# Activations and weights in two DMA queues at the start of a two-block network

## The chip, the core and the metric

The kernel runs on one NeuronCore of a Trainium2 chip. Its engines are TensorE (matrix products, PE in the profile; PEld is its loading of stationary operands), VectorE (DVE), ScalarE (ACT), GpSimd (POOL) and SyncE (SP, which here only issues DMAs). The metric is the device time of one execution in microseconds, less is better; the median of three runs is compared.

## The reference

For one sequence of 256 tokens of width 1024 in float32, two blocks run one after the other. The first has two layers: retention with four heads, then causal latent attention, each with a gated addition of a side input. The second has a gated convolution branch, a pooling branch and a feed-forward part. Only the very beginning matters here:

```
h = rms_norm(x, pre_norm_g[0])
z = h @ ret_w_in            # columns: q, k, v, gate
v = z[..., 2048:4096]       # four heads of 512 columns
q = rope(q, positions); k = rope(k, positions) / 16
```

rms_norm divides each token's row by the root of its mean square and multiplies by a gain per channel. The kernel multiplies by the gain first, and divides after the product, since the division is by token.

## The kernel before, in words

Activations are held transposed: 128 channels in the partitions, 256 tokens along the free dimension, so that x is eight blocks of 128 x 256 (`xt`, in two tiles of four blocks). Weights come as 128 x 128 or 128 x 512 blocks, packed on the host in the order of use into tiles of 128 x 1024 (512 KB), and are fetched by `fetch` (line 162, tile `raw`). For most products each operand is split in a rounded high part and a low rest, and three products of the fast float32 format (lines 234 to 236, `mm`) stand for one. The split of a weight tile is line 175 on ScalarE (`wh`, the high part) and line 176 on VectorE (`wl`, the rest). The split of an activation block with its gain is line 187 on ScalarE and line 188 on VectorE.

The first product is v of head 0 (`ret_v(0)`). Its eight weight blocks of 128 x 512 lie in four raw tiles of two blocks each. The first tile is not split: blocks 0 and 1 of x, times the gain (`xg`, line 497 on VectorE), meet the raw weights in full float32 products (line 240, `mm32`), for which the profile has two instructions each. For blocks 2 to 7 the split forms are used:

```
for kb in range(f):                                   # f = 2, full float32
    for b in range(2):
        mm32(psv[b], xg[kb][:, b * P:(b + 1) * P], v0raw[kb // 2][...], kb == 0, False)
for kb in range(f, 8):                                # three products each
    w = seq.next()                                    # splits the next raw tile
    for b in range(2):
        mm(psv[b], (xp[0][kb][:, bs], xp[1][kb][:, bs]), w, kb == 0, kb == 7)
```

Before the first product TensorE multiplies a tile of ones by itself nine times into a bank that nobody reads (line 273). The squares of x are taken in pairs of blocks on ScalarE (line 295), added on VectorE (line 299) and summed over the partitions by TensorE (line 359). `vec` is one tile of 458 columns with all gains, biases and small vectors; its first 16 columns are `pre_norm_g`. From the other columns, six small VectorE instructions (lines 661, 731, 732 and three of line 944) make scaled copies for later use, and the last two columns hold the rotary frequencies (line 441).

All early loads go out from SP in this order: vec, blocks 0 and 1 of x, the two halves of the first weight tile, blocks 2 and 3, the second weight tile, blocks 4 and 5, blocks 6 and 7, the third weight tile, the positions. They are held in program order. The order of all other instructions on each engine is settled at build time by a planner that weighs priorities, operands and expected times; on the chip each engine then runs its list strictly in that order. An instruction waits for the regions of a tile that it reads, not for the whole tile.

The profile calls loads of x `half<-in_xT`, loads of weights `raw<-in_wts`.

Of the kernel before, what the change touches and what calls it, by code (L numbers as in the profile page):

```python
# [21 lines left out]
D = 1024  # L22
# [60 lines left out]
def tile_kernel(ctx, tc, order, xT, pT, pos, vec, cst, cv, wada, wts, outT):  # L83
    nc = tc.nc
# [11 lines left out]
    def nm(s):  # L96
        uid[0] += 1
        return f"{s}_{uid[0]}"

    def bank():  # L100
        return pp.tile([P, 512], F32, tag="bank", name=nm("ps"))
# [52 lines left out]
    def fetch(entries, width, parts=True, step=D, pinned=False):  # L154
        g = len(order)
        order.append((width, list(entries)))
        n = len(entries) * width
        tag, bufs = (("raw", 6), ("wh", 5), ("wl", 5))[0 if parts else [0, 1][g % len([0, 1])]]
        raw = wp.tile([P, D], F32, tag=tag, name=nm("raw"), bufs=bufs)
        for o in range(0, n, step):  # L160
            e = min(n, o + step)
            d = nc.sync.dma_start(out=raw[:, o:e], in_=wts[g, :, o:e])
            if pinned:
                tc.keep_in_program_order(d)
        return raw[:, :n]
# [81 lines left out]
    xt = Blk(DB)  # L247
    vc = cp.tile([P, NV], F32, name="vec")
    posi = tp.tile([P, S], I32, tag="t1", name="posi", bufs=7)
    cs = cp.tile([P, NC], F32, name="cst")  # L250
    def load_x(q):
        tc.keep_in_program_order(nc.sync.dma_start(out=xt.pair(q), in_=xT[:, 2 * q:2 * q + 2, :]))


    v0 = [("ret_in", kb * P, 2048) for kb in range(8)]
    tc.keep_in_program_order(nc.sync.dma_start(out=vc, in_=vec))
    load_x(0)
    v0raw = []
    for q in range(3):
        v0raw.append(fetch(v0[2 * q:2 * q + 2], 512, q >= 1, 512 if q == 0 else D, True))  # L260
        if q < 2:
            load_x(q + 1)
        if q == 1:
            load_x(3)
    tc.keep_in_program_order(nc.sync.dma_start(out=posi, in_=pos.partition_broadcast(P)))
    ident = cp.tile([P, P], F32, name="ident")
    make_identity(nc, ident)
# [1 line left out]
    V.memset(ones, 1.0)  # L269

    wu = bank()
    for _ in range(9):
        T.matmul(wu[:, :P], ones, ones, start=True, stop=True)
    eps_r = cp.tile([P, 1], F32, name="eps_r")
    V.memset(eps_r, RMS_EPS)
# [387 lines left out]
    def post(x, ys, sums, layer, prepared):  # L663

        x1 = Blk(DB)

        def scaled(ks):
            for k in ks:
                A.activation(x1[k], ys.at(k), AF.Copy, scale=pgh[:, layer * 8 + k:layer * 8 + k + 1])
        scaled(range(3))  # L670
        nry = rms_neg2(sums.ps[0], D)
        scaled(range(3, DB))
        prj = prepared()
        x1p = two(DB)
        for k, n in ((0, 1), (1, 1), (2, 2), (4, 2), (6, 1), (7, 1)):
            V.tensor_mul(x1.span(k, n), x1.span(k, n), bc2(nry, n))
            V.tensor_add(x1.span(k, n), x1.span(k, n), x.span(k, n))
            split(x1p[0].span(k, n), x1p[1].span(k, n), x1.span(k, n))
        x2 = Blk(DB)

        def fin(ps, k, n):
            sgm = t2()[:, :n, :]
            A.activation(sgm, ps, AF.Sigmoid)
            V.tensor_mul(sgm, sgm, prj.span(k, n))
            V.tensor_add(x2.span(k, n), sgm, x1.span(k, n))

        half_outer(f"ple_gate{layer}", x1p, fin)
        return x2
# [38 lines left out]
    xt = post(xt, ys, sums, 0, prep)  # L727
# [200 lines left out]
    xt = post(xt, ys, sums, 1, prep)  # L928
# [508 lines left out]
```

## Time and profile before

| what | value |
|---|---|
| median of three runs | 865.53 us (865.46 to 867.07) |
| the profiled execution: its time | 866.75 us |
| its span, first to last instruction | 864.9 us |
| mean granted TensorE clock in it | 0.995 |
| PE busy | 848.1 us, 98% of the span |
| DVE busy | 710.0 us, 82% |
| ACT busy | 557.5 us, 64% |
| moved by DMA | 165.95 MB, 192 GB/s in the mean |

A row of a timeline has the start, the time taken, the engine, the line, the operation, what it writes and reads, and how many such instructions follow each other; in brackets the idle time of the engine before it and what ended that. In the chain of work that ended last, each piece starts when the one before it has released it. The granted clock of TensorE has two levels, 1.2 and 2.4 GHz. The column of the granted clock stands at 1.00 in the first microseconds too, where no change of the clock was recorded yet; what the engine had there is read from the spacing of equal instructions.

### The profile page before, as it was taken

How to read it: one execution, taken by the hardware profiler on the slowest of the kernel's cores; microseconds unless marked ns; L12 is line 12 of the kernel's file. 1: busy time of each engine (PE TensorE's matmuls, PEld its weight loads, DVE VectorE, ACT ScalarE, POOL GpSimd, SP SyncE). 2: the span in 40 equal slices, each digit the busy share in tenths (PEclk: the TensorE clock that was granted, in tenths of full speed). 3: DMA queues.
4: the chain of work that ended last, by engine and by line, in shares of the span. 5: the costliest groups of instructions: out<-in, count | busy, mean ns of one | idle time of the engine just before them, and what ended most of it. 6: DMA issues, size and time to landing. Idle time of an engine off the chain costs nothing.

```text
span 864.9 us, 16461 instructions
## 1 busy us (share of the span) xinstructions
PE 848.1 (98%) x6472; PEld 818.8 (95%) x6472; DVE 710.0 (82%) x1277; ACT 557.5 (64%) x943; POOL 4.2 (0%) x22
## 2 busy tenths in 40 slices
PE   8999999999999999999999999999999999999994
PEld 6989899999999999999999999999998999999993
DVE  6999787888888978799874768899776888889965
ACT  6665555445775785776744867998755776666533
POOL 0000000000000000000000000000000000000000
PEclk9999999999999999999999999999999999999997
DMA  9857556888556655465254364255473466567601
GB/s 333 314 217 243 196 206 207 271 258 297 170 185 228 225 185 199 160 227 197 97 183 171 122 219 152 92 170 185 137 239 124 135 187 191 185 230 256 206 27 49
DMA packets 46461, 165.95 MB, mean 192 GB/s; under 512 B 5168, under 2 KB 5936, under 8 KB 46384
## 3 DMA queue, kind: packets, MB, share of 16 engines
q1 hardware_dynamic: 46224, 164.39, 56.0%
q8 instruction: 50, 0.82, 0.4%
q0 software_dynamic: 160, 0.52, 0.2%
q14 instruction: 27, 0.22, 0.1%
HBM read 163.85 MB, written 1.05 MB: 191 GB/s over the span
## 4 chain that ended last, share of the span: by engine, by line
PE 95%; DVE 2%; DMA 2%; ACT 0%; issue 0%; SPq 0%; DVEq 0%
PE ps L235 27%; PE ps L234 27%; PE ps L236 27%; PE ps L240 10%; PE ps L359 2%; PE ps L337 1%; DMA adach<-in_wada 1%; DMA half<-in_xT 1%; PE ps L895 1%; PE ps L194 1%; DVE wl L176 0%; DVE t L1233 0%; DVE t L1230 0%; PE ps L1143 0%; PE ps L1151 0%
## 5 line engine op out<-in xcount | busy, mean ns | idle before, releaser
L234 PE MATMUL ps<-half,wh 128*128 128x256 f32 x1680 | 474.5, 283 | 0.0
L235 PE MATMUL ps<-half,wh 128*128 128x256 f32 x1680 | 472.9, 282 | 0.1
L236 PE MATMUL ps<-half,wl 128*128 128x256 f32 x1680 | 471.3, 281 | 0.0
L175 ACT CAST wh<-raw 128x1024 fp32r<-128x1024 f32 x233 | 242.6, 1048 | 159.7 <-PE ps L235 121.1
L176 DVE TENSOR_TENSOR wl<-raw,wh 128x1024 fp32r<-128x1024 f32 x233 | 282.4, 1222 | 64.3 <-ACT wh L175 62.5
L235 PEld LDWEIGHTS ps<-half,wh 128*128 128x128 f32 x1680 | 316.4, 188 | 1.6 <-DVE half L185 0.7
L236 PEld LDWEIGHTS ps<-half,wl 128*128 128x128 f32 x1680 | 316.9, 189 | 0.0
L234 PEld LDWEIGHTS ps<-half,wh 128*128 128x128 f32 x1680 | 316.0, 188 | 0.8
L240 PE MATMUL ps<-half,raw 128*128 128x256 f32 (+2 forms) x384 | 84.9, 380 | 0.0
L240 PEld LDWEIGHTS ps<-half,raw 128*128 128x128 f32 x384 | 72.5, 190 | 10.0
L409 DVE CUSTOM_DVE_ANT_0 adach<-adach,siluc 128x1024 f32<-128x1024 f32 x48 | 58.5, 1222 | 18.1 <-DMA adach<-in_wada 18.1
L1060 ACT ACTIVATE t<-apad,vec 128x256 f32<-128x256 f32 x106 | 44.4, 499 | 0.9 <-DVE half L1061 0.9
L1061 DVE TENSOR_TENSOR half<-half,t 128x512 f32<-128x512 f32 x53 | 36.7, 693 | 4.1 <-ACT t L1060 1.8
L234 PE MATMUL ps<-wh,half 128*128 128x512 f32 (+1 forms) x92 | 33.5, 366 | 0.0
L184 ACT CAST half<-t 128x256 fp32r<-128x256 f32 (+1 forms) x47 | 20.6, 453 | 19.7 <-DVE t L1323 12.1
L235 PE MATMUL ps<-wl,half 128*128 128x512 f32 (+1 forms) x92 | 32.7, 355 | 0.5 <-DVE wl L176 0.5
L236 PE MATMUL ps<-wh,half 128*128 128x512 f32 (+1 forms) x92 | 32.6, 355 | 0.0
L185 DVE TENSOR_TENSOR half<-t,half 128x256 fp32r<-128x256 f32 (+1 forms) x47 | 21.8, 485 | 3.7 <-ACT half L184 2.9
L1318 ACT ACTIVATE t<-ps,vec 128x256 f32<-128x256 f32 x38 | 21.0, 557 | 3.6 <-DVE t L1320 2.4
L235 PEld LDWEIGHTS ps<-wl,half 128*128 128x128 f32 x92 | 17.4, 189 | 3.3 <-DVE wl L176 1.0
L234 PEld LDWEIGHTS ps<-wh,half 128*128 128x128 f32 x92 | 17.3, 189 | 3.1 <-ACT wh L175 0.9
L236 PEld LDWEIGHTS ps<-wh,half 128*128 128x128 f32 x92 | 17.3, 188 | 2.6
(261 smaller groups left out, 994.6 us busy)
## 6 DMA issues: line engine op xcount, KB each, us to landing
raw<-in_wts SPq DMA_DIRECT2D x257, 512.0 KB, 4.2
adach<-in_wada SPq DMA_DIRECT2D x48, 512.0 KB, 4.8
half<-in_xT SPq DMA_DIRECT2D x4, 256.0 KB, 6.9
cst<-in_cst SPq DMA_DIRECT2D x1, 928.0 KB, 10.0
raw<-in_wts SPq DMA_DIRECT2D x2, 256.0 KB, 4.5
siluc<-in_cv SPq DMA_DIRECT2D x1, 512.0 KB, 8.1
t<-in_pT POOLq DMA_DIRECT2D x2, 256.0 KB, 4.9
out<-half SPq DMA_DIRECT2D x4, 128.0 KB, 2.0
```

The lines of the kernel that those rows point to most:

```text
L175: A.copy(hi, raw)
L176: V.tensor_sub(lo, raw, hi.bitcast(F32))
L184: A.copy(hi, src)
L185: V.tensor_sub(lo, src, hi.bitcast(F32))
L234: T.matmul(ps, l[0], r[0], start=first, stop=False)
L235: T.matmul(ps, l[0], r[1], start=False, stop=False)
L236: T.matmul(ps, l[1], r[0], start=False, stop=last)
L240: T.matmul(ps, w, r, start=first, stop=last)
L409: V.tensor_tensor_reduce(ch, ch, sc, 1.0, 0.0, MUL, ADD, mod[:, n:n + 1])
L1060: A.activation(t[:, b, :], apad[:, i0 + b, k:k + S], AF.Copy, scale=w[b])
L1061: V.tensor_add(acc.pair(i0 // 2), acc.pair(i0 // 2), t)
L1318: A.activation(t[:, b, :], ps[:, b, :], AF.Identity, bias=col("b_dw_f_2", m), scale=w[2])
```

## The change

The loads of x move from SP's queue to the one of ScalarE, as five transfers: block 0, block 1, blocks 2 and 3, 4 and 5, 6 and 7. SP first loads the 16 columns of `vec` that hold `pre_norm_g`, then the three weight tiles (the first in two halves, as before), then the other 442 columns of `vec`, then the positions. TensorE does seven products of ones for nine.

```diff
-    def load_x(q):
-        tc.keep_in_program_order(nc.sync.dma_start(out=xt.pair(q), in_=xT[:, 2 * q:2 * q + 2, :]))
+    def load_x(k, n):
+        tc.keep_in_program_order(nc.scalar.dma_start(out=xt.span(k, n), in_=xT[:, k:k + n, :]))
 
     v0 = [("ret_in", kb * P, 2048) for kb in range(8)]
-    tc.keep_in_program_order(nc.sync.dma_start(out=vc, in_=vec))
-    load_x(0)
-    v0raw = []
-    for q in range(3):
-        v0raw.append(fetch(v0[2 * q:2 * q + 2], 512, q >= 1, 512 if q == 0 else D, True))
-        if q < 2:
-            load_x(q + 1)
-        if q == 1:
-            load_x(3)
+    tc.keep_in_program_order(nc.sync.dma_start(out=vc[:, :16], in_=vec[:, :16]))
+    for k, n in ((0, 1), (1, 1), (2, 2), (4, 2), (6, 2)):
+        load_x(k, n)
+    v0raw = [fetch(v0[2 * q:2 * q + 2], 512, q >= 1, 512 if q == 0 else D, True) for q in range(3)]
+    tc.keep_in_program_order(nc.sync.dma_start(out=vc[:, 16:], in_=vec[:, 16:]))
     tc.keep_in_program_order(nc.sync.dma_start(out=posi, in_=pos.partition_broadcast(P)))
...
     wu = bank()
-    for _ in range(9):
+    for _ in range(7):
         T.matmul(wu[:, :P], ones, ones, start=True, stop=True)
```

## Rows read from the trace of the kernel before

**Rows 1.** The page's part on the chain of work that ended last: its share of the span by engine.

```profile
PE 95%; DVE 2%; DMA 2%; ACT 0%; issue 0%; SPq 0%; DVEq 0%
```

**Rows 2.** The chain that ended last, in order of time, from 0 to 30 us: start, time taken, engine or DMA, tile and line.

```profile
2.59 6.37 DMA half<-in_xT
8.98 0.91 ACT half L187 x2
...
10.61 0.94 ACT wh L175
11.58 1.24 DVE wl L176
12.86 0.50 PE ps L235
...
15.43 1.81 PE ps L359 x8
```

**Rows 3.** Who waited for whom, TensorE's products, whole execution: engine, tile, line, what it waited for, us in total, times, longest.

```profile
PE ps L895 <- DVE sm L884: 1.0, 1, 1.0
PE ps L337 <- DVE t L346: 0.9, 1, 0.9
...
PE ps L235 <- DVE wl L176: 0.5, 1, 0.5
```

**Rows 4.** Timeline of TensorE's products, 0 to 16 us.

```profile
1.05 4.21 PE L273 MATMUL ps<-ones 128*128 128x128 f32 x18 [1.05 <-DVE eps_l L277]
6.06 5.50 PE L240 MATMUL ps<-raw,half 128*128 128x512 f32 x8 [0.80 <-DMA raw<-in_wts]
11.60 0.73 PE L234 MATMUL ps<-wh,half 128*128 128x512 f32 x2
```

**Rows 5.** Timeline of TensorE's loads of stationary operands, 0 to 13 us, four of line 240.

```profile
8.75 0.34 PEld L240 LDWEIGHTS ps<-raw,half 128*128 128x128 f32 x1 [0.52 <-issue]
9.60 0.26 PEld L240 LDWEIGHTS ps<-raw,half 128*128 128x128 f32 x1 [0.52 <-issue]
10.11 0.19 PEld L240 LDWEIGHTS ps<-raw,half 128*128 128x128 f32 x1 [0.24 <-issue]
10.54 0.19 PEld L240 LDWEIGHTS ps<-raw,half 128*128 128x128 f32 x1 [0.24 <-issue]
```

**Rows 6.** Timeline of SP's DMA issues, 0 to 60 us, the first ones.

```profile
0.74 0.38 SPq L256 DMA_DIRECT2D vec<-in_vec  x1
1.18 0.42 SPq L252 DMA_DIRECT2D half<-in_xT  x1
1.65 0.90 SPq L162 DMA_DIRECT2D raw<-in_wts  x2
2.59 0.43 SPq L252 DMA_DIRECT2D half<-in_xT  x1
3.06 0.43 SPq L162 DMA_DIRECT2D raw<-in_wts  x1
...
4.82 0.61 SPq L162 DMA_DIRECT2D raw<-in_wts  x1
```

**Rows 7.** The same loads one by one, each from the DMA view of the stretch that holds its issue alone, in the order of issue (at 0.74, 1.18, 1.65, 2.11, 2.59, 3.06 and 4.82 us): size, us from issue to landing.

```profile
vec<-in_vec SPq DMA_DIRECT2D x1, 229.0 KB, 2.5
half<-in_xT SPq DMA_DIRECT2D x1, 256.0 KB, 3.7
raw<-in_wts SPq DMA_DIRECT2D x1, 256.0 KB, 4.3
raw<-in_wts SPq DMA_DIRECT2D x1, 256.0 KB, 4.8
half<-in_xT SPq DMA_DIRECT2D x1, 256.0 KB, 6.4
raw<-in_wts SPq DMA_DIRECT2D x1, 512.0 KB, 7.2
...
raw<-in_wts SPq DMA_DIRECT2D x1, 512.0 KB, 8.1
```

**Rows 8.** Table by stretches, 2 to 9 and 9 to 13 us: stretch, length, busy time (and instructions) of PE, PEld, DVE, ACT and POOL, granted clock, busy share of the 16 DMA engines, GB/s.

```profile
2.00:9.00 7.00, 6.21 (x20) 4.39 (x19) 2.04 (x10) 1.65 (x6) 0.01 (x1) 1.00 0.91 283
9.00:13.00 4.00, 3.43 (x8) 1.18 (x8) 3.00 (x5) 4.00 (x9) 0.00 (x0) 1.00 1.04 414
```

**Rows 9.** Timeline of ScalarE, 0 to 24 us.

```profile
0.73 1.28 ACT L278 ACT_TABLE_LOAD   x1 [0.73 <-PEq L1420]
...
4.94 0.63 ACT L295 ACTIVATE t<-half 128x512 f32<-128x512 f32 x1 [2.72 <-DMA half<-in_xT]
...
8.98 0.91 ACT L187 ACTIVATE half<-half,vec 128x256 fp32r<-128x256 f32 x2 [2.61 <-DMA half<-in_xT]
...
10.51 1.03 ACT L175 CAST wh<-raw 128x1024 fp32r<-128x1024 f32 x1
11.45 1.70 ACT L187 ACTIVATE half<-half,vec 128x256 fp32r<-128x256 f32 x4
```

**Rows 10.** Timeline of VectorE, 0 to 24 us.

```profile
3.31 0.18 DVE L661 TENSOR_SCALAR pgh<-vec 128x16 f32<-128x16 f32 x1 [2.29 <-DMA vec<-in_vec]
...
3.53 0.31 DVE L944 TENSOR_SCALAR lng<-vec 128x8 f32<-128x8 f32 x3
...
9.52 0.89 DVE L188 SCALAR_TENSOR_TENSOR half<-half,vec,half 128x256 fp32r<-128x256 f32 x2 [2.64 <-ACT half L187]
```

## The prediction

> **What bounds the kernel now.** I read the shares of the chain that ended last first, since they tell whether the start can matter at all: 95% of it is TensorE [rows 1]. Then the waits of TensorE's products over the whole execution [rows 3]: after the first microseconds only two waits of note are left, 1.0 us at line 895 and 0.9 us at line 337, each behind a short chain of this kernel's own that moves with TensorE. So from the first split product on TensorE runs almost without a gap, and the kernel ends earlier by what that steady run starts earlier. Third, the chain through the first 30 us [rows 2]: the steady run starts at 12.86 us with the first line 235. Going back from there: the low part of the second weight tile (line 176, from 11.58), its high part on ScalarE (line 175, critical from 10.61, started 10.51 [rows 9]), ScalarE's work on blocks 2 and 3 of x from 8.98 on, and the load of these blocks, issued at 2.59 and 6.37 us under way. Two loads are nearly tied there: blocks 2 and 3 land at 8.99 (2.59 + 6.4), the second weight tile at 10.26 (3.06 + 7.2) [rows 6, 7]; the cast starts 0.25 us after that landing, because ScalarE still has line 187 and what follows it in its list.
>
> TensorE before that is not the bound. Its warm-up ends at 5.26, it waits 0.80 us for the first half tile of weights, runs the eight full float32 instructions from 6.06 to 11.56, and then does two line 234 and stops for the low part [rows 4]. The spacing of those eight tells the clock: 0.85 us from 8.75 to 9.60, 0.43 us from 10.11 to 10.54 [rows 5]. So the engine had 1.2 GHz until shortly after 9.60, after the warm-up, the gap of 0.80 and some 3.5 us of products, and 2.4 GHz from then on.
>
> Last, the loads. From 2 to 9 us the DMA engines are 91% busy and move only 283 GB/s, from 9 to 13 us 414 GB/s [rows 8]. So a load's landing follows from the bytes ahead of it, on a curve that is slow at first. In KB up to and with each load, and its landing from [rows 6, 7]: vec 229 at 3.24; blocks 0 and 1, 485 at 4.88; half tiles 741 at 5.95 and 997 at 6.91; blocks 2 and 3, 1253 at 8.99; second tile 1765 at 10.26; third tile, with 512 KB of x in between, 2789 at 12.92.
>
> **The change, part by part.**
>
> *The order of bytes.* 221 KB of vec go behind the third weight tile; 8 KB stay in front. The two queues share the engines. How they are mixed no row shows, so I bound it. Packets of x are half as wide as those of weights (128 KB against 256, 256 against 512 for as many rows), so if the engines alternate packet by packet from the same start, each load of x ends with the weight load next to it. Then the second weight tile has 8 + 512 + 256 + 512 + 256 = 1544 KB up to its end: 8.99 + 291 KB x 2.48 ns (slope between 1253 and 1765) = 9.71 us. If the small vec transfer holds SP back by one step, blocks 4 and 5 run beside it: 1800 KB, 10.35. I take the middle, 10.03 (before: 10.26). Blocks 2 and 3 land at 7.2 us in the second pairing (1032 KB) and at 9.7 in the first; the first half tile at 4.28 (392 KB) or 5.03 (520 KB), against 5.95.
>
> *From there to the steady run.* Cast start to first line 235 took 12.86 - 10.51 = 2.35 us, and that stays. If ScalarE is free, the cast starts 0.1 us after the landing. The bounds: 9.71 + 0.1 + 2.35 = 12.16 (gain 0.70); 10.35 + 0.1 + 2.35 = 12.80 (gain 0.06); and in the first pairing with the cast behind ScalarE's work on blocks 2 and 3 (10.51 - 8.98 = 1.53 us), 9.71 + 1.53 + 2.35 = 13.59 (loss 0.73). The middle, 10.03 + 0.1 + 2.35 = 12.48, gains 0.4 us, and this I take.
>
> *Two products of ones fewer.* Eighteen instructions took 4.21 us, the last starting near 4.84, so 0.223 us from one to the next; fourteen end near 4.4. The first weights come at 4.3 to 5.0, so TensorE starts its real products at 4.4 to 5.1, a gap of 0 to 0.7 us against 0.80 [rows 4]. From 5.1, with the clock rising at the same 9.7, eight instructions end at about 10.9 (5.4 at 0.853, 2.6 at 0.43); at 1.2 GHz throughout at 11.95. Both lie before 12.16. So this part costs and brings nothing by itself; it is covered by the wait for the second tile, and if that wait goes, each of those instructions left at the low clock costs 0.43 us.
>
> *Five issues on ScalarE.* At 0.43 us each, or up to 0.6 where issues back up [rows 6], they take 2.2 to 3 us before the table load (1.28 us, [rows 9]), so ScalarE is ready at about 4.4 to 5.2, not at 2.2. Its first work started at 4.94, after 2.72 us idle, and another 2.61 us idle stand before 8.98. Costed at nothing. Without that cover the split of blocks 0 and 1 is late, which TensorE does not read in this product.
>
> *Four issues fewer on SP, one more.* The second weight tile is issued near 2.1 for 3.06, the third near 2.5 for 4.82. With up to 7 to 8 us from issue to landing [rows 7], it is the bytes ahead that set the landing. Bytes up to the third tile and vec together are 2789 KB as before, so positions and everything behind them land as before.
>
> *Six small VectorE instructions.* They ran from 3.31 to 3.84 [rows 10] because vec was the first load. Their columns now land with 2789 KB, 12.92 us. So 0.53 us moves into a stretch in which VectorE is full. Cover: blocks 2 to 5 come earlier in half of the cases, and VectorE sat idle 2.64 us before 9.52 [rows 10]. I take nothing, with 0.53 us as the upper bound.
>
> The Trainium skill, page "DMA: Bandwidth & Descriptors", section "Issuing engines are not separate DMA queues", says that transfers of different issuing engines interleave on the same 16 DMA engines, and that a second issuer saves only issue time. By that rule the gain is that of the byte order alone, as summed above, and the second rival below does not exist. The row with 91% busy at 283 GB/s fits engines that are short of data rather than of work, and does not decide it [rows 8].
>
> **Sum.** The profiled execution has 866.75 us, of which 864.9 are the span; minus 0.4 gives 866.35. It lies 1.2 us above the median of the runs, so for the median I forecast 865.53 - 0.4 = 865.1 us. A change within 0.2% (1.7 us) is about what this kernel's runs cannot tell from none; their own spread is 1.6.
>
> **The rivals.**
>
> *Hidden by the sums.* TensorE's list has the sums of squares (line 359) at 15.43, on the chain [rows 2]. They need blocks 6 and 7, which end the queue of x at about 2568 KB, 12.35 us by the curve, while ScalarE's four line 187 ran from 11.45 [rows 9]. Then the sums come no earlier than now, and TensorE waits there for what it gained: 865.5.
>
> *The slow start is eased.* If a second queue lets the DMA engines overlap their slow first reads, and they move 414 GB/s instead of 283 over those 7 us, the same 1.98 MB take 4.8 us and the second tile lands 2.2 us sooner, 7.8. The steady run could start at 10.25, but the eight first products end at 10.5 to 10.9: gain 2.0, 863.5. Half of it gives 864.0. For it: the engines are slow while busy. Against: nothing shows that queues are what they lack.
>
> *VectorE blocked (slower).* If the six small instructions stand ahead of the first line 176 in VectorE's list, it waits for 12.92, does 0.53 us of them, starts line 176 at about 13.55 and TensorE at 14.83: 1.97 us later, 867.5. It decides from that place in the list alone; ahead of line 497 it would be over 4 us. For it: before, they stand ahead of all. Against: they stood there because vec was first.
>
> *The clock falls (slower).* TensorE is through at 9 to 10.9 and stands until 12.2 to 12.5 but for two products. If the clock falls to 1.2 GHz for as long as it was low after 6.06 (3.7 us), half is lost, 1.84 us: 865.1 + 1.8 = 867.0. Before, a shorter stop there left the clock high.
>
> **How the numbers follow.** Forecast 0.50 (its own range 864.8 to 866.3, from the bounds -0.70 and +0.73); hidden 0.14; eased start 0.20; VectorE blocked 0.11; clock 0.05. Faster by over 0.2% comes from the eased start and the tail of the forecast, 0.20; slower from the last two, 0.14; the rest, 0.66, is within. The range 863.4 to 867.0 takes in the eased start, the bounds and the clock, and leaves most of the blocked VectorE outside.
>
> **What would show it.** Right: the first line 240 at 4.4 to 5.1, the first line 235 at 12.2 to 12.8, the second weight tile landing at 9.7 to 10.4, line 661 near 13 us and behind the first line 176. Wrong: DMA well above 283 GB/s before 9 us, a cast that waits behind line 187, line 240 instructions spaced 0.85 us to their end, or a new wait at line 359.

## The result, and the profile after

| | before | changed |
|---|---|---|
| median | 865.50 us | 871.98 us (870.53 to 872.93, six runs) |
| ratio, 95% interval | | 1.0070 (1.0057 to 1.0084) |
| profiled execution, time and span | 866.75 and 864.9 us | 872.30 and 870.5 us |
| mean granted TensorE clock | 0.995 | 0.992 |

The change costs 6.5 us, 0.7%, and the range of the prediction ended at 867.0. Lines behind the loads now stand two lower than before: line 293 is the old 295 (squares), 297 the old 299 (their additions), 357 the old 359 (sums), 659 the old 661.

First the chain that ended last, as shares of the span by engine, which stands against 95% for TensorE in [rows 1]:

```profile
PE 86%; DVE 7%; DMA 5%; issue 1%; ACT 0%; SPq 0%; ACTq 0%; DVEq 0%
```

Next the same chain in order of time (start, time taken, engine or DMA, tile and line); [rows 2] is its counterpart.

```profile
15.66 1.22 PE ps L357 x2
16.88 0.85 PE ps L234 x2
17.73 0.67 PE ps L235
18.40 0.43 PE ps L236
...
22.60 0.24 PE ps L235
```

The steady run began with line 235 at 12.86 us before. Now line 235 comes at 17.6, behind two sums of squares. Its products stand 0.43 us apart at first, and 0.23 to 0.24 us apart from 22 us on. So there is a late start, and a slow stretch behind it. The waits of TensorE (us in total, times, longest) show the late start as one wait, and its timeline says where:

```profile
PE ps L357 <- DVE t L297: 6.0, 1, 6.0
```

```profile
1.06 3.21 PE L271 MATMUL ps<-ones 128*128 128x128 f32 x14 [1.06 <-DVE eps_l L275]
5.46 1.96 PE L240 MATMUL ps<-raw,half 128*128 128x512 f32 x4 [1.20 <-DMA raw<-in_wts]
7.67 1.96 PE L240 MATMUL ps<-raw,half 128*128 128x512 f32 x4 [0.25 <-DMA raw<-in_wts]
15.66 1.22 PE L357 MATMUL ps<-t,ones 128*128 128x256 f32 x2 [6.04 <-DVE t L297]
17.61 0.79 PE L235 MATMUL ps<-wl,half 128*128 128x512 f32 x1
```

The eight full float32 instructions are through at 9.63 us, earlier than the 11.56 of [rows 4]. Then TensorE stands for 6.04 us.

What was ready in that time? The second weight tile was issued at 2.12 us and took this long (size, us from issue to landing):

```profile
raw<-in_wts SPq DMA_DIRECT2D x1, 512.0 KB, 7.3
```

It landed at 9.42 us, 0.8 earlier than the 10.26 before. Its cast to the high part did not start then. ScalarE's timeline from its table load on:

```profile
4.15 1.28 ACT L276 ACT_TABLE_LOAD   x1 [4.15 <-DMA half<-in_xT]
...
5.54 0.90 ACT L187 ACTIVATE half<-half,vec 128x256 fp32r<-128x256 f32 x2
7.74 0.91 ACT L187 ACTIVATE half<-half,vec 128x256 fp32r<-128x256 f32 x2 [1.29 <-DMA half<-in_xT]
9.87 0.91 ACT L187 ACTIVATE half<-half,vec 128x256 fp32r<-128x256 f32 x2 [1.22 <-DMA half<-in_xT]
11.66 0.51 ACT L187 ACTIVATE half<-half,vec 128x256 fp32r<-128x256 f32 x1 [0.88 <-DMA half<-in_xT]
...
12.67 2.17 ACT L293 ACTIVATE t<-half 128x512 f32<-128x512 f32 x4
14.75 3.87 ACT L175 CAST wh<-raw 128x1024 fp32r<-128x1024 f32 x4
```

With the weight tile landed, ScalarE waits for blocks 4 and 5 of x until 9.87 and again for blocks 6 and 7 until 11.66, splits all eight blocks, makes all four squares, and only then casts, 5.33 us after the landing. An engine works through its list in order, and the list is not the one of before. The beginning of the two lists as the planner wrote them (split of a block of x: line 187; square of a pair: 295 or 293; cast of a weight tile: 175; a tile of zeros: 280 or 278; table loads and a copy of one column left out):

```
before: 295, 187 x4, 295, 280, 175 (second tile), 187 x4, 295, 295, 175 (third tile), ...
after:  DMA x5, 187 x7, 278, 187, 293 x4,         175 (second tile), 175 (third tile), ...
```

The source orders none of these; the planner does. TensorE's list changed in the same sense (two sums now stand ahead of the first split product), and so did VectorE's. From VectorE's timeline:

```profile
12.13 0.17 DVE L659 TENSOR_SCALAR pgh<-vec 128x16 f32<-128x16 f32 x1 [0.83 <-DMA vec<-in_vec]
...
14.92 0.69 DVE L297 TENSOR_TENSOR t<-t,t 128x512 f32<-128x512 f32 x1
...
16.33 1.22 DVE L176 TENSOR_TENSOR wl<-raw,wh 128x1024 fp32r<-128x1024 f32 x1
```

The delay of the first line 235 adds up from these: the cast starts 14.75 - 10.51 = 4.24 us later than in [rows 9]; from cast to low part 16.33 - 14.75 = 1.58 us pass where it was 11.58 - 10.51 = 1.07, 0.51 more, because VectorE still works through its list; from low part to line 235 it is 1.28 us in both. 4.24 + 0.51 = 4.75 = 17.61 - 12.86.

The rest is the clock. A table by stretches (stretch, length, busy time and instructions of PE, PEld, DVE, ACT and POOL, granted clock, busy share of the DMA engines, GB/s):

```profile
9.60:15.60 6.00, 0.02 (x1) 0.00 (x0) 4.22 (x15) 4.85 (x10) 0.00 (x0) 0.89 1.04 404
15.60:22.00 6.40, 6.34 (x17) 4.76 (x18) 6.40 (x13) 6.37 (x8) 0.00 (x0) 0.57 1.03 410
22.00:29.00 7.00, 7.00 (x34) 5.77 (x33) 6.57 (x12) 4.57 (x7) 0.00 (x0) 1.00 1.02 414
```

While TensorE stood, its clock fell: the mean is 0.89 in the wait and 0.57 in the stretch after it, where TensorE is busy for 6.34 of 6.40 us but does 17 instructions. By the spacing, 1.2 GHz held from line 235 at 17.61 to the sum at 20.96; at half speed that loses 3.35 / 2 = 1.7 us. Together 4.75 + 1.7, less some 0.46 us (two sums at 0.23) that now are done ahead of line 235, is 6.0 us. The chain's last steps come 5.97 us later (the step of line 1237 at 860.56 is that of line 1235 at 866.53). So the loss between these two executions is as large as that of the first 21 us; in between they are not always 6 us apart, to which the section on the prediction comes back.

### The profile page after: what moved, and what is told of

Its sections match the earlier page's. It is cut to its first block, busy times and chain, and to the rows that moved or that the text cites. A ratio compares the mean times of both kernels' runs of the same rounds, so it can differ in the third digit from the quotient of the medians.

```text
span 870.5 us, 16457 instructions
## 1 busy us (share of the span) xinstructions
PE 848.2 (97%) x6468; PEld 819.0 (94%) x6468; DVE 710.2 (82%) x1277; ACT 558.0 (64%) x943; POOL 4.2 (0%) x22
## 4 chain that ended last, share of the span: by engine, by line
PE 86%; DVE 7%; DMA 5%; issue 1%; ACT 0%; SPq 0%; ACTq 0%; DVEq 0%
PE ps L235 24%; PE ps L236 24%; PE ps L234 24%; PE ps L240 10%; DMA adach<-in_wada 4%; DVE wl L176 2%; PE ps L357 2%; PE ps L335 1%; DVE adach L407 1%; DMA posi<-in_pos 1%; PE ps L893 1%; DMA half<-in_xT 0%; PE ps L194 0%; DVE half L185 0%; DVE t L1231 0%
## 5 line engine op out<-in xcount | busy, mean ns | idle before, releaser
L357 PE MATMUL ps<-t,ones 128*128 128x256 f32 x72 | 18.2, 391 | 6.0 <-DVE t L297 6.0
L357 PEld LDWEIGHTS ps<-t,ones 128*128 128x128 f32 x72 | 13.7, 197 | 8.9 <-DVE t L297 6.9
```

Source lines behind the costliest of these rows:

```text
L357: T.matmul(ps, ones, pairs[k // 2][:, k % 2, :], start=(k == 0), stop=(k == n - 1))
```

## The experiments

The theory after the result: the second tile came sooner, as was forecast, and the planner's new lists, ScalarE's above all, cost what is lost. The rivals: the second queue itself (the loads, the issues on ScalarE), the later columns of `vec`, the shorter warm-up, or TensorE's list. Medians in us, each beside the kernel before in the same series:

| kernel | median | before | ratio (95%) |
|---|---|---|---|
| after's loads, lists mended | 865.35 | 866.36 | 0.9992 (0.9979 to 1.0006) |
| after's loads, only TensorE's list mended | 872.75 | 866.39 | 1.0069 (1.0049 to 1.0088) |
| before's loads, cast placed late | 867.14 | 866.36 | 1.0015 (1.0003 to 1.0028) |
| only x in a second queue | 869.95 | 866.36 | 1.0044 (1.0029 to 1.0058) |
| only `vec` in two parts | 866.65 | 866.36 | 1.0003 (0.9994 to 1.0012) |
| only seven warm-up products | 865.96 | 866.22 | 0.9999 (0.9990 to 1.0008) |
| after with nine warm-up products | 869.93 | 866.22 | 1.0050 (1.0033 to 1.0067) |
| after, with products that fill the wait | 871.15 | 866.22 | 1.0054 (1.0035 to 1.0073) |
| mended, sums and squares last | 870.07 | 866.22 | 1.0045 (1.0033 to 1.0058) |
| mended, squares early, VectorE free | 867.87 | 866.39 | 1.0012 (0.9999 to 1.0026) |
| the same, VectorE's list mended too | 864.45 | 866.39 | 0.9978 (0.9966 to 0.9989) |
| that one's lists, loads in one queue | 866.09 | 866.39 | 0.9997 (0.9985 to 1.0009) |

### One part alone

Three kernels made one part of the change each. Only x in ScalarE's queue (`vec` whole, nine warm-up products):

```diff
-        tc.keep_in_program_order(nc.sync.dma_start(out=xt.pair(q), in_=xT[:, 2 * q:2 * q + 2, :]))
+        tc.keep_in_program_order(nc.scalar.dma_start(out=xt.pair(q), in_=xT[:, 2 * q:2 * q + 2, :]))
```

> One part alone: the kernel before with the four loads of x in ScalarE's queue; vec stays whole and first, nine warm-up products. Order theory: ScalarE's list has the cast behind all of x here too, so 869.5 to 872. If instead the late columns of vec were the cause: 865.5.

It is 0.44% slower. ScalarE's and TensorE's timelines show the changed kernel's picture: the cast comes behind all squares, and TensorE stands for 3.38 us.

```profile
12.27 2.17 ACT L295 ACTIVATE t<-half 128x512 f32<-128x512 f32 x4
14.35 3.88 ACT L175 CAST wh<-raw 128x1024 fp32r<-128x1024 f32 x4
```

```profile
15.71 0.70 PE L359 MATMUL ps<-t,ones 128*128 128x256 f32 x2 [3.38 <-DVE t L299]
...
17.18 0.50 PE L235 MATMUL ps<-wl,half 128*128 128x512 f32 x1 [0.55 <-DVE wl L176]
```

Its interval and that of the whole change touch (1.0058 and 1.0057). So this part has most of the loss; whether it has all of it is open.

Only `vec` in two parts, everything in SP's queue:

```diff
-    tc.keep_in_program_order(nc.sync.dma_start(out=vc, in_=vec))
+    tc.keep_in_program_order(nc.sync.dma_start(out=vc[:, :16], in_=vec[:, :16]))
...
+    tc.keep_in_program_order(nc.sync.dma_start(out=vc[:, 16:], in_=vec[:, 16:]))
```

> Another part alone: the kernel before with one queue and nine warm-up products, but 16 columns of vec first and the other 442 behind the third weight tile. Order theory: the cast stays right behind blocks 2 and 3, the second weight tile has 221 KB fewer ahead of it and lands some 0.5 us sooner, so 865.0 (864.5 to 865.5). If the late columns block VectorE: 866 or more.

The same time as before, and not the 864.5 to 865.5 expected. Here ScalarE's list keeps the cast between the blocks, at 9.30 us and 1.2 us earlier than before; the first line 235 follows at 11.64. But the gain does not reach the end: 20 us later TensorE waits for a low part.

```profile
31.94 0.38 PE L236 MATMUL ps<-half,wl 128*128 128x256 f32 x1 [1.33 <-DVE wl L176]
```

The time is the one expected if the late columns block VectorE, but they do not block it here: the first of the small instructions runs at 13.89 us, and the first low part had begun at 10.36. What else differs near 32 us is TensorE's list: 24 products stand there that the kernel before has later. Whether they cost the 1.33 us was not tried.

Only seven warm-up products, and the change with nine of them:

```diff
-    for _ in range(9):
+    for _ in range(7):
```

> The kernel before with seven warm-up products for nine, all else as before. The products end 0.9 us sooner and TensorE waits 1.7 us instead of 0.8 for the first weights. Order theory: the same as before, 865.5 to 866.4; if the warm-up's length matters for the clock, 1 us or more slower.

> The changed kernel with nine warm-up products again. If the two products fewer have a part in the loss, 1 us or more comes back; order theory: nothing does, 870.5 to 872.5.

Seven for nine makes no difference to the kernel before. With nine the changed kernel keeps its late cast (14.97 us) and its wait at line 357 (5.8 us); its median is 0.6 us under the range expected, and its interval overlaps that of seven, so nothing is told apart between them.

So the move of x to another queue put the cast behind all of x, and the other two parts did not.

### The lists mended, and spoilt

The changed kernel's loads with the order put back by hand: the second tile's cast is written ahead of the split of block 4 and held there, and the sums are held behind the products of block 3.

```diff
         for b in range(DB):
-            split(pair[0][b], pair[1][b], x[b], col("pre_norm_g", layer * 8 + b))
+            if layer == 0 and b == 4:
+                early.append(load(v0[2:4], 512, True, v0raw[1]))
+            split(pair[0][b], pair[1][b], x[b], col("pre_norm_g", layer * 8 + b), pin=layer == 0 and b == 4)
...
-            sum_mm(ps, sq)
+            sum_mm(ps, sq, pin=layer == 0)
```

> The changed kernel with all its loads, but with the lists of two engines mended: ScalarE's cast of the second weight tile (the first that is split) stands right behind the split of x's blocks 2 and 3 again, and ahead of blocks 4 to 7 and of the squares; TensorE's sums of squares stand behind the products of blocks 2 and 3 again. Order theory (the loss is the new order of these lists): the cast starts within 0.2 us of the landing of that tile, 9.4 to 9.6 us, the first low-part product (line 235 of the kernel before) at about 11.9 against 12.86, no stretch at 1.2 GHz after 10 us, time 864.5, and at most 865.5. Load theory (two queues disturb the loads): the loads land as in the changed kernel and the time stays at 870 or more.

The loss is gone. The cast starts at 9.60, the first product on the low part at 11.96 us (here line 241), 0.9 earlier than before. More than it gained it waits off at the sums (line 363): of TensorE's products the 6400th from the end starts at 23.99 us, against 22.85 before. The time is that of before all the same; the last product is 0.7 us earlier (851.81 against 852.52), and in this execution the wait of line 895 in [rows 3], 1.0 us, does not occur.

```profile
PE ps L363 <- DVE t L303: 1.9, 1, 1.9
```

Was it TensorE's list or ScalarE's? With the last edit of that diff alone, TensorE's list is mended and the others stay:

> The changed kernel with TensorE's list alone mended: all sums behind products of block 3, none in front of the first split product; ScalarE's list stays as changed, the cast behind all of x. If ScalarE's list makes the loss: the cast starts near 14.7 as in the changed kernel, and the time stays at 870 to 872. If the sums in front of the products make it: 866.5 or less.

```profile
15.76 1.22 PE L234 MATMUL ps<-wh,half 128*128 128x512 f32 x2 [6.03 <-ACT wh L175]
```

The wait is as long as in the changed kernel, with another name: now TensorE waits for the cast. So with the cast late the two sums ahead cost nothing by themselves, and the name in the row of the wait (line 297) was the last of several. ScalarE's list alone was not mended; what the two sums cost with a cast in time is not shown.

The reverse test puts the cast late with the loads of before:

```diff
-        A.copy(hi, raw)
+        i = A.copy(hi, raw)
+        if not seen:
+            tc.keep_in_program_order(i)
+            seen.append(1)
```

> The kernel before with all its loads, and one thing pinned: the cast of the second weight tile stands behind all splits and squares of x in ScalarE's list, as in the changed kernel. Order theory: the cast starts near 14.2 us, when the squares are done, instead of 10.51, the first low-part product near 16.5 instead of 12.86; TensorE does its 1.7 us of sums while it waits, so some 2 us are lost, and up to 2.4 more if the clock falls in the stop: 867.5 to 870. Load theory: the loads are those of before, so 865.5.

It loses, but 0.15% and not 0.7%. The timeline of its profiled execution (866.86 us) says why:

```profile
13.07 1.13 PE L364 MATMUL ps<-t,ones 128*128 128x256 f32 x4 [1.40 <-DVE t L304]
...
14.50 1.02 PE L364 MATMUL ps<-t,ones 128*128 128x256 f32 x4
15.18 0.58 PE L240 MATMUL ps<-wl,half 128*128 128x512 f32 x1
15.60 0.40 PE L241 MATMUL ps<-wh,half 128*128 128x512 f32 x1
15.83 0.40 PE L240 MATMUL ps<-wl,half 128*128 128x512 f32 x1
```

The eight float32 instructions end at 11.67 here, the cast comes at 12.72 (10.51 before, 14.75 in the changed kernel; 14.2 was expected, but its loads landed sooner), and all eight sums fit into what would be a wait. TensorE stands for 1.40 us and not for 6, and its clock stays up: the products behind the first on the low part start at 15.60 and 15.83 us, 0.23 apart. That holds for this execution: the ten took 865.32 to 870.25 us, and two with a mean granted clock of 0.991, for 0.995 in the profiled one, took 868.46 and 869.37. What a late cast costs depends on how long TensorE then stands, on what else its list can do, and, as it seems, on whether the clock falls.

### The clock's share

The changed kernel with 24 products of ones, into the bank that nobody reads, between the float32 instructions and the first split product:

```diff
+        if h == 0:
+            for _ in range(24):
+                tc.keep_in_program_order(T.matmul(wu[:, :P], ones, ones, start=True, stop=True))
         for kb in range(f, 8):
```

> The changed kernel with 24 more products of ones by ones, of which nothing is read, between the eight full float32 instructions and the first split product, so that TensorE works through the stop and its clock has no reason to fall. ScalarE's list is that of the changed kernel. If the fallen clock is a part of the loss: line 235 starts near 17.6 as in the changed kernel, equal products stand 0.23 us apart and not 0.43, and the time falls by some 2 us, from about 871.5 to 869.5. If the stop alone makes the loss: 871.5.

```profile
10.86 5.52 PE L526 MATMUL ps<-ones 128*128 128x128 f32 x48
...
17.48 0.50 PE L235 MATMUL ps<-wl,half 128*128 128x512 f32 x1 [0.21 <-DVE wl L176]
```

The same stretches as above, granted clock in the seventh place:

```profile
9.60:15.60 6.00, 6.00 (x47) 5.28 (x46) 4.35 (x15) 4.89 (x10) 0.00 (x0) 1.00 1.04 398
15.60:22.00 6.40, 6.19 (x31) 5.00 (x31) 6.40 (x13) 6.37 (x8) 0.00 (x0) 1.00 1.03 406
```

The clock stays at 2.4 GHz, the products behind line 235 stand 0.23 us apart, and v of head 0 is done 1.7 us sooner (of TensorE's products, the 6400th from the end starts at 26.98 instead of 28.71 us; 22.85 before). So the price of the clock at this place is shown. In the median it does not show: 869.5 was expected, and 871.15 has an interval that overlaps the changed kernel's. Of the 1.7 us the span of the profiled executions keeps 0.6 (869.9 against 870.5). The engines' lists are those of the changed kernel but for the 24 products and a handful of instructions, and two waits of TensorE are there that the changed kernel has at 0.2 us (the first) or not at all:

```profile
PE ps L335 <- DVE t L325: 0.8, 1, 0.8
PE ps L896 <- DVE sm L885: 0.7, 1, 0.7
```

Line 896 here is line 895 of [rows 3], 1.0 us before; its instructions lie between 319 and 453 us. So 0.6 + 0.7 of the 1.7 us are lost again there. That it is because these chains do not come earlier with TensorE is not shown: the kernel before with seven warm-up products has the lists of the kernel before on TensorE, ScalarE and VectorE but for those two products, is 0.10 us behind it at the 6400th product (22.95 us) and 0.78 at the last (853.30), with waits of its own in the same stretch. Differences of this size between two executions need no edit.

### A better order for these loads

With the loads mended, the sums are the next wait. Two ways around it were tried. The first gives the first layer's squares a later due time, so that they and the sums stand behind all of v's products:

```diff
-        after(3.33, squares)
+        after(6.2 if layer == 0 else 3.33, squares)
```

> The kernel with mended lists (e1_order), and the squares of x with their sums placed behind all products of v of head 0, so that the 1.9 us for which TensorE waited there at the sums go too. If that wait hid what the new loads gain: the time falls by 1 to 1.9 us under that of e1_order, to about 864, a gain of 0.2% or more on the kernel before. If another wait takes its place (low parts of the third tile, the scale of v): 865 to 866.

```profile
PE ps L363 <- DVE t L303: 3.2, 1, 3.2
```

Worse, and outside both cases expected: the wait grows to 3.2 us, since ScalarE makes the squares only from 21.63 us on, and the clock falls behind it (granted clock 0.57 in the mean from 25 to 29 us):

```profile
25.00:29.00 4.00, 4.00 (x17) 3.44 (x16) 3.04 (x6) 2.98 (x4) 0.00 (x0) 0.57 1.02 408
```

The second takes the opposite way: the squares of blocks 0 to 3 stand right behind their splits, in time in which ScalarE waits for loads anyway, then the cast, then blocks 4 to 7.

```diff
+            if layer == 0 and b in (1, 3):
+                first.append(t2())
+                tc.keep_in_program_order(A.activation(first[-1], x.pair(b // 2), AF.Square))
```

> As e13_best, but without the pins on VectorE: its list has the reading of the positions, two copies from the late columns of vec and one rotary product ahead of the first low part (line 176 of the kernel before). If VectorE stands at them until those loads land, near 12.9: the low part starts near 13.7 instead of 10.7, the first low-part product near 15 instead of 11.9, 2 to 3 us over e13_best, so 866 to 867. If VectorE is not held: as e13_best.

VectorE's and TensorE's timelines of this one:

```profile
13.04 0.29 DVE L442 CAST t<-posi 128x256 f32<-128x256 int32 x1 [3.27 <-DMA posi<-in_pos]
```

```profile
14.94 0.79 PE L241 MATMUL ps<-wl,half 128*128 128x512 f32 x1 [3.67 <-DVE wl L180]
```

ScalarE's cast is in time (9.44 us), and now VectorE's list holds the cast of the positions ahead of the low part: it waits 3.27 us for their load, TensorE 3.67 for VectorE, and the products behind stand 0.43 us apart. This profile is of the longest of the ten executions (869.35 us, mean granted clock 0.991); the three shortest took 865.33 to 865.97 at 0.996, so the wait does not cost as much in each. The last step holds VectorE's early instructions where the source has them, and moves the positions' cast behind the splits:

```diff
-    V.tensor_copy(posf, posi)
...
     xp = prenorm(xt, 0, have_r0)
+    tc.keep_in_program_order(V.tensor_copy(posf, posi))
...
-    V.tensor_scalar(pgh, col("post_norm_g", 0, 16), -0.5, None, MUL)
+    tc.keep_in_program_order(V.tensor_scalar(pgh, col("post_norm_g", 0, 16), -0.5, None, MUL))
```

> All loads of the changed kernel, and the lists as the landings in its trace suggest: on ScalarE the squares of blocks 0 to 3 each behind their splits (it sits idle there), then the cast of the second weight tile, then blocks 4 to 7 with their squares, then the cast of the third; on VectorE the instructions that read the late columns of vec behind the low part of the second tile or far later; TensorE as before. Against e1_order the squares take 1.2 us less behind the cast, so the wait at the sums falls from 1.9 to about 0.7 us. If the order of the lists was all that stood against the new loads: first low-part product near 11.9, time 863.5 to 864.5, some 2 us under the kernel before. If the rest of the kernel gives it back: 865 to 866.

```profile
11.94 0.50 PE L241 MATMUL ps<-wl,half 128*128 128x512 f32 x1 [0.35 <-DVE wl L180]
...
14.37 1.96 PE L366 MATMUL ps<-t,ones 128*128 128x256 f32 x8
```

The sums follow without a wait, and the kernel is 0.22% faster than the one before, which none of the others is. In the trace 0.95 us of that are there at the 6400th product from the end (21.90 against 22.85 us) and 2.26 at the last one (850.26 against 852.52); of the rest, 1.0 us is the wait of line 895 [rows 3], which this execution does not have. How much of the gain is the second queue, and how much the lists? The same lists with the loads in one queue (`vec` in two parts, nine warm-up products):

> The lists of e13_best on the loads of one queue (16 columns of vec first, the rest of vec late, x and weights alternating in SP's queue, nine warm-up products). If a second queue brings nothing that the order of bytes does not bring: the second weight tile lands at 9.2 to 9.7 and the time is that of e13_best within 0.5 us. If the second queue is worth something by itself: 1 us or more slower than e13_best.

```profile
11.51 0.50 PE L241 MATMUL ps<-wl,half 128*128 128x512 f32 x1 [0.53 <-DVE wl L180]
...
310.88 0.39 PE L242 MATMUL ps<-half,wl 128*128 128x256 f32 x1 [0.94 <-DVE wl L180]
```

866.09 against 864.45 (865.03 to 868.62 against 863.29 to 866.37); the intervals of the two ratios still touch (0.9985 and 0.9989). The start does not explain it. Up to 18 us the lists are the same but for the loads and the two products of ones, and with one queue the first product on the low part comes 0.43 us sooner and the 6400th from the end 0.22 us sooner (21.68 against 21.90 us). The traces part later, above all at 310.88 us, where TensorE waits 0.94 us with one queue and not at all with two. This wait is not tied to the queues: it is 0.58 us in the changed kernel and 2.19 with nine warm-up products, whose lists are otherwise the same. So the second queue brings nothing at the start; whether the 1.6 us between the medians are its doing, and how, stays open.

## Why the prediction was wrong

**The step that failed** is "From there to the steady run": "If ScalarE is free, the cast starts 0.1 us after the landing." The cast started 5.33 us after it. The bound for the bad case had the cast "behind ScalarE's work on blocks 2 and 3", 13.59 us, and came short by 4.0 us (17.61), because it took the list of before for given: there the cast stands behind blocks 0 to 3, and the sum moved only the landings. The planner works the list out anew, and with x in a queue of its own it has all of x and its squares ahead of the weights, with this part of the change alone too. By what it chose that order no run shows. The two times in the sum hold once the list is mended: the tile lands at 9.6 us (2.11 + 7.5) and the cast starts at 9.60, and from there to the first product on the low part it is 2.36 us, for 2.35. What failed is the place in the list, and behind it the clock, which cost another 1.7 us. "A cast that waits behind line 187" was named as the sign of a wrong forecast, but no rival was made of it, with a place and a price. [rows 9] held the hint: the cast stood behind line 187 of just those blocks whose load stood ahead of it in the queue. Of the four signs of being right none came.

**The order of bytes** had the right direction, and both bounds were too late: the second tile landed at 9.42 us, forecast 9.71 to 10.35. When the lists are mended, the first product on the low part comes at 11.96 and 11.94 us, forecast 12.48 with a lower end of 12.16. The curve of landings was that of one execution. The same tile, issued at 3.06 us in the kernel with the cast late, whose loads are those of before, and at 3.07 in the one with only `vec` in two parts:

```profile
raw<-in_wts SPq DMA_DIRECT2D x1, 512.0 KB, 6.3
raw<-in_wts SPq DMA_DIRECT2D x1, 512.0 KB, 6.1
```

So with the loads of before it can land at 9.4 us too, 0.9 sooner than in [rows 7], and with one queue and `vec` behind it at 9.2, sooner than with two. The second queue did not bring the tile forward; `vec` may have.

**The products of ones** cost nothing, as forecast (0.9999). Fourteen ended at 4.27 (forecast 4.4); the first weights let line 240 start at 5.46, outside 4.4 to 5.1, which the wait behind it covered.

**The issues on ScalarE** ended 3.38 us after the first began, and the table load behind them ended at 5.43, where ScalarE was to be ready at 4.4 to 5.2. The issues themselves are as forecast, 1.86 us for four and 0.33 for the fifth; the sum had no term for the 1.19 us that lie between, a wait on which the last section has more. With the lists mended ScalarE waits for its loads in spite of that (0.83 us ahead of the cast), so they are free.

**The six VectorE instructions** landed where the rival had them, ahead of the first line 176 (line 659 at 12.13). They did not hold it, since the cast was later still; they share in the 0.51 us that VectorE took off its list between cast and low part. The mechanism itself, VectorE blocked by a late load ahead of the low part, is shown by the kernel with VectorE free, though for the load of the positions and not for `vec`: 3.67 us of waiting there, and the lower clock behind it.

**Hidden by the sums** came true as a wait when the lists were mended, 1.9 us at line 363 with a ratio of 0.9992, but not for the reason given. The landing of blocks 6 and 7 does not hold the sums: with the same loads the kernel that is 0.22% faster than the one before has them at 14.37 us without a wait. It is the lists of ScalarE and VectorE that made them late.

**"Without a gap"**, the reading that the waits of [rows 3] sit behind chains that move with TensorE, is not borne out. The changed kernel is 5.9 us behind at the end of v of head 0 and 5.97 at the end, but 7.2 in between (the 4000th product from the end starts at 337.65 us, against 330.45): it waits 0.58 us at line 236 at 317.77, and the kernel before then waits 1.0 us at line 895, which the changed one does not. That the two ends agree is in part luck. And such waits come and go with the same lists, as the two executions show in which line 236 waits 0.58 and 2.19 us.

**The slow start eased** is false. The stretch from 2 to 9 us in the changed kernel, to set against [rows 8]:

```profile
2.00:9.00 7.00, 5.56 (x19) 3.43 (x18) 2.31 (x6) 3.19 (x6) 0.01 (x1) 1.00 0.93 299
```

299 GB/s for 283, not 414; all kernels with two queues have 299 to 328 in these 7 us, those with one 269 to 295. The Trainium skill's page "DMA: Bandwidth & Descriptors", section "Issuing engines are not separate DMA queues", had spoken against this rival: issuing engines share the same DMA engines. The traces agree in the main, with 0.93 busy for 0.91 here and a few per cent between the two sorts of kernels.

**The clock falls** came true, with a price close to the forecast (1.84 us, measured 1.7) and a chance of 0.05, which was given for a stop between 9 to 10.9 and 12.2 to 12.5 us. The stop was 6.04 us. That the prices agree is luck: the forecast took its 3.7 us from another stretch, in which the clock had not yet risen. The row of 1.40 us of standing in the kernel with the late cast shows a stop that did not cost the clock in that execution.

## What to carry to other kernels

Where a planner orders the engines' lists, a load that moves to another queue moves more than bytes: compare the lists of both kernels, engine by engine, before the sum, and treat the place of each instruction on the critical chain as part of the change. A wait's row names what came last; when one list is mended, the same wait can come back under another name, so mend the engine that ends the chain and look again. A start that comes sooner is worth only what the next join lets through: here the sums of squares, and a low part 20 us later. And before a difference between two traces is put down to an edit, look how far two executions with the same lists differ: here a single wait near 318 us was 0.58 us in one and 2.19 in another.

## What the runs showed that was not expected

**Loads of two queues wait for each other ahead of their issue.** SP issued the rest of `vec` at 5.53 us, after a wait for a load of x, which is in the other queue (SP's waits, changed kernel):

```profile
SPq L262 <- DMA half<-in_xT: 1.6, 1, 1.6
```

ScalarE's own fifth issue (blocks 6 and 7) waited too. The four before it end at 2.60 us; it starts at 3.79, when block 0 has landed, on which VectorE's first line 495 starts:

```profile
0.74 1.86 ACTq L254 DMA_DIRECT2D half<-in_xT  x4
3.79 0.33 ACTq L254 DMA_DIRECT2D half<-in_xT  x1
...
3.79 0.35 DVE L495 TENSOR_SCALAR half<-half,vec 128x256 f32<-128x256 f32 x1 [2.77 <-DMA half<-in_xT]
```

Nothing in the source asks for this. Eight loads of the two queues had gone out by 2.60 us, and each of the next three waited for a landing: these two, and the third weight tile, for which SP waited 1.0 us until the 16 columns of `vec` were there. That the program keeps eight completion counters for all loads and waits for an earlier load before it reuses one would explain it; it was not tried.

**The clock rose at different times.** Products stood 0.85 us apart until after 9.60 us before [rows 5] (the clock column reads 1.00 there, so the spacing decides). In the changed kernel the first four of line 240 run at 2.4 GHz already: they take 1.96 us from 5.46 on, where eight took 5.50 us in [rows 4]. The granted clock then fell while TensorE stood between 9.63 and 15.66 us, and the spacing became 0.23 us again only at about 21 us, with products since 15.66: most of what the stop cost in clock was paid after it had ended.
